# Gate/up results turned by DMA transposes on 16-bit planes instead of by TensorE

## The chip, the cores and the metric

One Trainium2 chip, one of its cores. The metric is the device time of one execution in microseconds, of which the median over several runs is taken. The program is compiled once; its weights lie in HBM and stream through the core's SBUF during the execution. TensorE (PE) multiplies, VectorE (DVE) and ScalarE (ACT) prepare its operands and take its results, SyncE (SP) issues most DMAs, ScalarE and GpSimd (POOL) issue some from their own queues. Each engine runs its instructions strictly in program order and waits on semaphores.

## The reference, cut to what matters

One layer of an encoder with 512 tokens and 2048 channels in fp32: two attention mixers side by side, an output projection, then a SwiGLU feed-forward of width 5632 (44 columns of 128) and a final RMSNorm. The change touches the hand-over inside the feed-forward:

```python
h2 = rmsnorm(x, g_ffn[layer])
gate, up = jnp.split(jnp.einsum('bsd,df->bsf', h2, w_gate_up[layer]), 2, axis=-1)
x = x + jnp.einsum('bsf,fd->bsd', jax.nn.silu(gate) * up, w_down[layer])
```

`silu(gate) * up` comes out with tokens on the partitions, and the product with `w_down` needs it with its 5632 columns on the partitions. It has to be turned, in blocks of 128 by 128.

## The kernel before, in words

**Products.** Every fp32 product is made from two-part operands: a value is split into a rounded first half (`hi`, by ScalarE, a Copy to the matmul's fp32r type) and the rest (`lo`, by VectorE, a subtraction), and `mm3` (lines 220 to 224) adds three matmuls, hi x hi, hi x lo and lo x hi. On top of that, `ColBlock` (line 841) uses a 2 x 2 block scheme with seven products instead of eight. The seven are called forms, `m1` to `m7`; each takes a sum of activation blocks (made ahead, in `arena`) and a sum of weight blocks (made when needed: `weights`, line 874, a VectorE step on two `raw` tiles, line 878).

**Units.** The program is a list of units. In the gate/up stage a unit is one form of one pair of 128 rows: six matmuls of 128 x 512. For unit n the generator emits, in this order: `prepare(n)` (line 1375), which loads weights for units up to `COLS_LOAD` = 20.0 planned us ahead and emits the splits of units up to `COLS_AHEAD` = 8.0 planned us ahead (a unit is planned at 1.37 us, so up to n + 5); the matmuls of unit n; and then the functions hooked to n. For each unit, `split_hi` (line 812) first makes the weight sum if the form needs one, then ScalarE writes the first half into the next `tw` pair (line 815); VectorE writes the second half (line 818), one unit behind the first halves. There are 8 `tw` pairs in turn (`TWINS`), so a first half waits until TensorE has finished the unit eight before.

**A gate/up block** (`gate_up_block`, line 1107) takes four of the 44 columns for gate and up, all 512 tokens, in 7 forms x 8 pairs = 56 units, in the order m1, m7, m6, m2, m5, m4, m3 (the first block has a part of it moved). Forms m7, m6, m5 and m4 need weight sums, m1, m2 and m3 do not. There are eleven blocks, one behind the other, then the down stage. The results gather in PSUM banks; `snap` copies them out after m1, m7 and m6 (line 1119, ScalarE), `add` adds m2, m5 and m4 (line 1126, VectorE), `silu` follows (line 1134), and after m3 `low` (line 1140) and `high` (line 1144) form the products `silu(gate) * up` of the two halves of the tokens, in the tiles `glo` and `uhi` (128 tokens x 512 columns, two tiles each).

**The turning** comes after m3, while TensorE is already in the next block: `turn(k)` for the four columns k, hooked to 6, 8, 18 and 20 units after the block's last unit. Each is four TensorE transposes of 128 x 128 into one bank (line 1151) and a copy of the bank by ScalarE (line 1154) into `pair`. Two columns make a pair; two units later `pair_sums` (four VectorE steps, line 353) forms the sums that the down stage's forms need, and `store` (line 1158) writes the seven forms to HBM from SP's queue. There is one `pair` tile, so the second pair's copies wait for the first one's store.

**Tiles.** Most tiles of the gate/up stage come from one set of interchangeable places, taken by `slot` (line 88, tag "s"); a tile waits for the last reader of what lay there before. Weights lie in `raw` tiles, 24 in the gate/up blocks.

Of the kernel before, what the change touches and what calls it, by code (L numbers as in the profile page):

```python
# [11 lines left out]
F32 = mybir.dt.float32  # L12
BF16 = mybir.dt.bfloat16
F32R = mybir.dt.float32r
AF = mybir.ActivationFunctionType
OP = mybir.AluOpType
AX = mybir.AxisListType
# [2 lines left out]
P = 128  # L20
# [51 lines left out]
def encoder_block(ctx, tc, x, w_in, g_q_a, g_k_a, w_out, w_gate_up, w_down, g_final, x_t, gains, c_ident, c_mask,  # L72
# [156 lines left out]
    units = []  # L229
    twins, evs, frs = [], [], []  # L230

    def in_turn(tiles, n, shape, dtype, tag):
        if not tiles:
            at_once = n if homing[0] else n // 2 if n == TWINS else 1
            for _ in range(n // at_once):
                whole = sp.tile([P, at_once] + shape[1:], dtype, tag=f"{tag}{at_once}", bufs=n // at_once, name=nm(tag))
                tiles.extend(whole[:, i] for i in range(at_once))
        tiles.append(tiles.pop(0))
        return tiles[-1]

# [743 lines left out]
    def out_chunk(kind, c):  # L984
        box = {}
        base = 0 if kind == "A" else NHA
        order = [6, 7, 0, 1, 2, 3, 4, 5] if (kind, c) == ("B", NC - 1) else list(range(NHA))

        def early(k):
            if (kind, k) not in oS and k >= SPILLED[kind]:  # L990
                drain_until(lambda: (kind, k) in oT)
                oS[kind, k] = split(oT.pop((kind, k)), "oS", go[:, base + k:base + k + 1],
                                    at=O_HOMES[kind][2 * k:2 * k + 2] if kind == "A" or k < 7 else None)

        class Back:
# [12 lines left out]
            def split_lo(self):  # L1008
                hi, lo = oS[kind, self.k]
                nc.vector.scalar_tensor_tensor(lo, self.t, go[:, base + self.k:base + self.k + 1], f32(hi),  # L1010
                                               op0=OP.mult, op1=OP.subtract)

        def mm(u, n):
            k = order[n]
            if n == 0:
                box["ps"] = [bank() for _ in range(NT)]
                if kind == "A":
                    x1[c] = [slot("x1") for t in range(NT)]
                    for t in range(NT):
                        nc.sync.dma_start(x1[c][t], x[0, t * P:(t + 1) * P, c * 512:(c + 1) * 512])  # L1020
            by_rows(u, n, NHA, lambda i, w, t: mm3(box["ps"][t], cols(oS[kind, order[i]], t * P), w, i == 0,
                                                   i == NHA - 1), post, kind == "A")

        def post(rows):
            drain_until(lambda: kind in ro)
            if (kind, c) == ("B", 0) and 0 in rows:
                nc.scalar.activation(slot("table")[:, :1], ones, AF.Silu)
            for t in rows:
                nc.vector.scalar_tensor_tensor(x1[c][t], box["ps"][t], ro[kind][:, t:t + 1], x1[c][t],
                                               op0=OP.mult, op1=OP.add)  # L1030
                release(box["ps"][t])
                if kind == "B" and c < NC - 1:
                    square_x1(c, t)
            if kind == "B" and NT - 1 in rows:
                wait(2 if c == 0 else 1)
                if c == NC - 1:
                    side.extend(lambda p=p: h_side(2 * c, p, True) for p in range(4))
                    side.append(lambda: [square_x1(c, t) for t in (0, 1)])
                    side.extend(lambda p=p: h_side(2 * c + 1, p, True) for p in range(2))
                    side.append(lambda: park_x1(c))  # L1040
                    side.append(lambda: [square_x1(c, t) for t in (2, 3)])
                    side.extend(lambda p=p: h_side(2 * c + 1, p, True) for p in range(2, 4))
# [64 lines left out]
    def gate_up_block(f0):  # L1107
        box = ColBlock(w_gate_up, 0, (f0 * P, DFF + f0 * P), KD // 2, REREAD, "craw40" if f0 == 40 else "craw", hf if f0 == 0 else None)
        st = {}

        def tile2(name):
            st[name] = slot(name, F32, (P, 2, 512))
            return st[name]

        def snap(form, name):
            def go():
                d = tile2(name)
                for t in range(2):
                    nc.scalar.activation(d[:, t], box.bank_of(form)[t], AF.Copy)
            box.after(form, 0, go)  # L1120

        def add(form, late, src, name):
            def go():
                d = st[name] = st.pop(src)
                for t in range(2):
                    nc.vector.tensor_tensor(d[:, t], box.bank_of(form)[t], d[:, t], op=OP.add)  # L1126
                if form in LAST_OF_BANK:
                    box.done(form)
            box.after(form, late, go)

        def silu(form, late, name, half):
            def go():
                for t in range(2):
                    nc.scalar.activation(st[name][:, t], st[name][:, t], AF.Silu,
                                         scale=r2["r"][:, 2 * half + t:2 * half + t + 1])
            box.after(form, late, go)

        def low():
            for t in range(2):
                nc.vector.tensor_tensor(st["glo"][:, t], box.bank_of("m3")[t], st["glo"][:, t], op=OP.mult)  # L1140
            box.done("m3")

        def high():
            nc.vector.tensor_tensor(st["uhi"], st["uhi"], st["ghi"], op=OP.mult)

        def turn(k):
            ps = bank()
            half = k % 2
            for n, t in enumerate((2, 3, 0, 1) if half == 0 else range(NT)):
                src = st[("glo", "uhi")[t // 2]][:, t % 2, k * P:(k + 1) * P]  # L1150
                nc.tensor.transpose(ps[:, n * P:(n + 1) * P], src, ident)  # L1151
# [24 lines left out]
        return box  # L1176

    for f in range(0, NFF, 4):
# [309 lines left out]
```

## Time and profile before

| | |
|---|---|
| median of 3 runs | 1971.99 us (1970.7 to 1972.68) |
| profiled execution, whole | 1972.09 us |
| its span, first to last instruction | 1970.3 us |
| the eleven gate/up blocks end | between 759 and 1541 us |
| TensorE, VectorE, ScalarE busy in 1072 to 1150 us (about one block) | 78.0, 63.4, 41.3 of 78 us |

The page gives busy times of each engine, the span in 40 slices, and the chain of work that ended last. Rows of groups read: line, engine, operation, tile written <- tiles read, partitions x elements, count | busy time, mean ns of one | idle time before it and what ended it. In a timeline, a row gives the start, the length, and the instruction; instructions that follow each other are put together with their count (x2), and overlap a little, so that two of them take less than twice one. The row of a window gives its length, then for each engine the busy time and (in brackets) the instructions, then the granted TensorE clock, the DMA engines' busy share and GB/s. Rows on DMA issues give the queue, the count, the size of each and the median us from issue to landing.

### The profile page before, as it was taken

How to read it: one execution, taken by the hardware profiler on the slowest of the kernel's cores; microseconds unless marked ns; L12 is line 12 of the kernel's file. 1: busy time of each engine (PE TensorE's matmuls, PEld its weight loads, DVE VectorE, ACT ScalarE, POOL GpSimd, SP SyncE). 2: the span in 40 equal slices, each digit the busy share in tenths (PEclk: the TensorE clock that was granted, in tenths of full speed). 3: DMA queues.
4: the chain of work that ended last, by engine and by line, in shares of the span. 5: the costliest groups of instructions: out<-in, count | busy, mean ns of one | idle time of the engine just before them, and what ended most of it. 6: DMA issues, size and time to landing. Idle time of an engine off the chain costs nothing.

```text
span 1970.3 us, 27367 instructions
## 1 busy us (share of the span) xinstructions
PE 1958.3 (99%) x8903; PEld 1615.1 (82%) x8903; DVE 1590.8 (81%) x2727; ACT 1126.1 (57%) x2045; POOL 120.3 (6%) x162
## 2 busy tenths in 40 slices
PE   9999999999999999999999999999999999999998
PEld 7888887888888888888888888888888888888886
DVE  7987678787775797787878878878879988878877
ACT  7755554565555565555554555545555666656655
POOL 0000011000000000000000000000000121111121
PEclk9999999999999999999999999999999999999999
DMA  9677683243343573754846737657457798869865
GB/s 343 234 258 235 211 272 111 69 138 124 131 148 119 183 240 130 275 197 172 299 137 221 275 123 259 226 171 276 160 193 273 205 270 247 233 144 265 236 131 167
DMA packets 230929, 399.01 MB, mean 203 GB/s; under 512 B 22785, under 2 KB 69633, under 8 KB 230657
## 3 DMA queue, kind: packets, MB, share of 16 engines
q1 hardware_dynamic: 205232, 330.84, 49.9%
q0 software_dynamic: 17200, 40.38, 9.4%
q10 hardware_dynamic: 8352, 26.05, 4.0%
q8 instruction: 69, 1.13, 0.2%
q14 instruction: 76, 0.61, 0.1%
HBM read 334.52 MB, written 62.65 MB: 202 GB/s over the span
## 4 chain that ended last, share of the span: by engine, by line
PE 92%; DVE 4%; ACT 1%; issue 1%; DMA 1%; ACTq 0%; DVEq 0%; POOLq 0%; SPq 0%; POOL 0%
PE b L222 30%; PE b L224 30%; PE b L223 30%; PE b L587 1%; PE b L1151 1%; DVE tw L818 1%; DMA raw<-in_w_down_dram 0%; DMA fr<-forms 0%; DVE raw L878 0%; PE b L1075 0%; DVE w L280 0%; PE b L537 0%; DVE arena L1202 0%; ACT tw L815 0%; DVE ra L434 0%
## 5 line engine op out<-in xcount | busy, mean ns | idle before, releaser
L222 PE MATMUL b<-tw,arena 128*128 128x512 f32 x2244 | 878.1, 391 | 0.6 <-ACT ev L1223 0.6
L223 PE MATMUL b<-tw,arena 128*128 128x512 f32 x2244 | 873.6, 389 | 0.6 <-DVE tw L818 0.6
L224 PE MATMUL b<-tw,arena 128*128 128x512 f32 x2244 | 874.0, 389 | 0.0
L815 ACT ACTIVATE tw<-raw 128x512 fp32r<-128x512 f32 x924 | 557.2, 628 | 426.5 <-DVE raw L878 290.8
L818 DVE TENSOR_TENSOR tw<-raw,tw 128x512 fp32r<-128x512 f32 x924 | 620.4, 686 | 161.9 <-ACT tw L815 151.9
L223 PEld LDWEIGHTS b<-tw,arena 128*128 128x128 f32 x2244 | 421.4, 188 | 88.1 <-DVE tw L818 1.7
L224 PEld LDWEIGHTS b<-tw,arena 128*128 128x128 f32 x2244 | 421.2, 188 | 88.4 <-DVE arena L321 0.4
L222 PEld LDWEIGHTS b<-tw,arena 128*128 128x128 f32 x2244 | 421.3, 188 | 87.7 <-ACT ev L1223 1.3
L878 DVE TENSOR_TENSOR raw<-raw,raw 128x512 f32<-128x512 f32 x528 | 360.9, 684 | 1.9 <-DMA raw<-in_w_gate_up_dram 1.9
L1224 POOL DMA_DIRECT2D x1d<-ev x76 | 66.3, 968 | 1144.5 <-ACT ev L1223 1127.4
L815 ACT ACTIVATE tw<-stage 128x512 fp32r<-128x512 f32 x140 | 85.4, 628 | 69.4 <-DVE stage L878 45.0
L818 DVE TENSOR_TENSOR tw<-stage,tw 128x512 fp32r<-128x512 f32 x140 | 93.8, 687 | 22.6 <-ACT tw L815 21.8
L222 PE MATMUL b<-w,arena 128*128 128x512 f32 x240 | 95.7, 399 | 0.0
L213 ACT ACTIVATE pTh<-b 128x512 fp32r<-128x512 f32 x64 | 38.2, 598 | 98.0 <-PE b L587 94.3
L224 PE MATMUL b<-w,arena 128*128 128x512 f32 x240 | 93.9, 391 | 0.0
L223 PE MATMUL b<-w,arena 128*128 128x512 f32 x240 | 93.5, 390 | 0.0
L1223 ACT ACTIVATE ev<-b,fixed 128x512 f32<-128x512 f32 x76 | 49.8, 682 | 29.1 <-PE b L224 27.3
L353 DVE TENSOR_TENSOR pair<-pair 128x256 f32<-128x256 f32 x120 | 45.5, 421 | 23.6 <-ACT pair L1078 22.6
L1126 DVE TENSOR_TENSOR s<-b,s 128x512 f32<-128x512 f32 x66 | 44.0, 687 | 24.7 <-PE b L224 24.7
L1154 ACT ACTIVATE pair<-b 128x512 f32<-128x512 f32 x44 | 26.3, 597 | 48.9 <-PE b L1151 48.6
L224 PEld LDWEIGHTS b<-w,arena 128*128 128x128 f32 x240 | 45.0, 188 | 10.0
L223 PEld LDWEIGHTS b<-w,arena 128*128 128x128 f32 x240 | 45.2, 188 | 9.1
(223 smaller groups left out, 1779.5 us busy)
## 6 DMA issues: line engine op xcount, KB each, us to landing
raw<-in_w_gate_up_dram SPq DMA_DIRECT2D x616, 256.0 KB, 5.3
raw<-in_w_down_dram SPq DMA_DIRECT2D x176, 256.0 KB, 6.4
stage<-in_w_in_dram SPq DMA_DIRECT2D x111, 256.0 KB, 5.3
forms<-pair SPq DMA_DIRECT2D x22, 896.0 KB, 5.3
x1d<-ev POOLq DMA_DIRECT2D x76, 256.0 KB, 6.5
fr<-forms ACTq DMA_DIRECT2D x35, 512.0 KB, 4.5
raw<-in_w_out_dram SPq DMA_DIRECT2D x32, 512.0 KB, 4.9
stage<-in_w_in_dram SPq DMA_DIRECT2D x90, 128.0 KB, 3.4
```

Source lines behind the costliest of these rows:

```text
L213: nc.scalar.activation(hi, src, AF.Copy)
L222: nc.tensor.matmul(dst, ah, bh, start=start, stop=False, skip_group_check=chained)
L223: nc.tensor.matmul(dst, ah, bl, start=False, stop=False, skip_group_check=chained)
L224: nc.tensor.matmul(dst, al, bh, start=False, stop=stop, skip_group_check=chained)
L353: nc.vector.tensor_tensor(out, x, y, op=op)
L815: nc.scalar.activation(self.pair[:, 0], self.src, AF.Copy)
L818: nc.vector.tensor_tensor(self.pair[:, 1], self.src, f32(self.pair[:, 0]), op=OP.subtract)
L878: nc.vector.tensor_tensor(t[dst], t[src[0]], t[src[1]], op=OP.add if form == "m6" else OP.subtract)
L1126: nc.vector.tensor_tensor(d[:, t], box.bank_of(form)[t], d[:, t], op=OP.add)
L1154: nc.scalar.activation(st["pair"][:, half * 1024:half * 1024 + 512], ps, AF.Copy)
L1223: nc.scalar.activation(e, box.bank_of(form)[t], AF.Copy, scale=r2["r"][:, row:row + 1])
L1224: nc.gpsimd.dma_start(x1_dram[2 * cb + j, row], e, accum_op=OP.add)
```

## The change

The transposes leave TensorE. `planes` (ScalarE) copies each of the four 128 x 512 results as 16-bit words, so that the lower and the upper words of each pair of columns lie apart (1024 words a partition), and issues from ScalarE's own DMA queue a transpose from SBUF to SBUF, 128 x 1024 words into 8 blocks of 128 x 128 (in the built program, tiles of 16 rows by 128 columns, so 64 a transfer). `merge(j)` (ScalarE, three copies) interleaves the words of two turned columns into `pair`. `planes` stands 2 and 4 units after the block's end, `merge` 9 and 19. `pair_sums` follows one unit after its merge, `store` six.

With that, three other things change. The `tw` pairs are single tiles from the attention stage on (class `Pair`), where they were cut from two tiles of four pairs each. Results and residuals (`s1` to `uhi`) are single 128 x 512 tiles rather than tiles of two, so `high` becomes two steps; the residual `x1` becomes one tile of four instead of four. And one of the 21 `raw` buffers of the first two column blocks of the down stage goes (`draw6` 21 to 20), which makes room.

```diff
-RAWS = {"raw": 6, "craw": 24, "craw0": 24, "kraw": 9, "craw40": 18, "draw6": 21, "draw8": 28}
+RAWS = {"raw": 6, "craw": 24, "craw0": 24, "kraw": 9, "craw40": 18, "draw6": 20, "draw8": 28}
...
+    class Pair:
+        def __init__(self):
+            self.parts = [sp.tile([P, 512], F32R, tag="tw", bufs=2 * TWINS, name=nm("tw")) for _ in range(2)]
+
+        def __getitem__(self, at):
+            return self.parts[at[1]]
...
         def tile2(name):
-            st[name] = slot(name, F32, (P, 2, 512))
+            st[name] = [slot(name) for t in range(2)]
             return st[name]
...
         def high():
-            nc.vector.tensor_tensor(st["uhi"], st["uhi"], st["ghi"], op=OP.mult)
-
-        def turn(k):
-            ps = bank()
-            half = k % 2
-            for n, t in enumerate((2, 3, 0, 1) if half == 0 else range(NT)):
-                src = st[("glo", "uhi")[t // 2]][:, t % 2, k * P:(k + 1) * P]
-                nc.tensor.transpose(ps[:, n * P:(n + 1) * P], src, ident)
+            for t in range(2):
+                nc.vector.tensor_tensor(st["uhi"][t], st["uhi"][t], st["ghi"][t], op=OP.mult)
+
+        def planes(name, half):
             if half == 0:
-                st["pair"] = sp.tile([P, 4 * 512], F32, tag="pair", bufs=1, name=nm("pair"))
-            nc.scalar.activation(st["pair"][:, half * 1024:half * 1024 + 512], ps, AF.Copy)
-            release(ps)
+                st["turned"] = sp.tile([P, NT, 2, 2, 2, P], U16, tag="turned", bufs=1, name=nm("turned"))
+            for t in range(2):
+                halves = slot("planes", U16, (P, 2, 2, 256))
+                src = st[name][t].bitcast(U16).rearrange("p (j c s) -> p j s c", j=2, s=2)
+                nc.scalar.activation(halves, src, AF.Copy)
+                nc.scalar.dma_start_transpose(st["turned"][:, 2 * half + t].rearrange("p j s f c -> p (j s f) c"),
+                                              halves.rearrange("p j s c -> p (j s c)"))
+            st.pop(name)
+
+        def merge(j):
+            pair = st["pair"] = sp.tile([P, 4 * 512], F32, tag="pair", bufs=1, name=nm("pair"))
+            turned = st["turned"][:, :, j].rearrange("p t s f c -> p f t c s")
+            for f, lo, hi, at in ((0, 2, 4, 0), (0, 0, 2, 256), (1, 0, 4, 1024)):
+                dst = pair[:, at:at + (hi - lo) * P].bitcast(U16).rearrange("p (t c s) -> p t c s", c=P, s=2)
+                nc.scalar.activation(dst, turned[:, f, lo:hi], AF.Copy)
...
-        for k in range(4):
-            late = (6, 8, 18, 20)[k]
-            box.after("m3", late, lambda k=k: turn(k))
-            if k % 2:
-                box.after("m3", late + 2, lambda: pair_sums(st["pair"]))
-                box.after("m3", late + 7, lambda k=k: store((f0 + k) // 2))
+        for late, name, half in ((2, "glo", 0), (4, "uhi", 1)):
+            box.after("m3", late, lambda name=name, half=half: planes(name, half))
+        for j, late in enumerate((9, 19)):
+            box.after("m3", late, lambda j=j: merge(j))
+            box.after("m3", late + 1, lambda: pair_sums(st["pair"]))
+            box.after("m3", late + 6, lambda j=j: store(f0 // 2 + j))
```

In the changed kernel the lines after 231 have other numbers: the splits are at 825 and 828, the weight sums at 888, the snaps at 1130, `low` at 1151, `high` at 1156, the plane copies at 1164, the transposes at 1165, the merges at 1174, `pair_sums` at 363, the store at 1177.

How ScalarE's program moves, after the end of the second block. Before (`tw` is a split of a coming unit, the snap of m1 is line 1119):

```order
L1154 ACTIVATE pair_7323<-b_74 128x512
L815 ACTIVATE tw_5865<-raw_7223 128x512
L815 ACTIVATE tw_5866<-raw_7235 128x512
L1154 ACTIVATE pair_7323<-b_73 128x512
L1119 ACTIVATE s_690_7348<-b_78 128x512
L1119 ACTIVATE s_690_7348<-b_77 128x512
L815 ACTIVATE tw_5866<-raw_7247 128x512
```

Now, first the planes, four units or more earlier than the first eviction was (the two splits between them are those of the next block's units 8 and 9):

```order
L1164 ACTIVATE planes_7292<-s_638_6710 128x1024
L1165 DMA_TRANSPOSE turned_7291<-planes_7292 128x8x128
L1164 ACTIVATE planes_7295<-s_639_6711 128x1024
L1165 DMA_TRANSPOSE turned_7291<-planes_7295 128x8x128
L825 ACTIVATE tw_5867<-raw_7181 128x512
L825 ACTIVATE tw_5853<-raw_7193 128x512
L1164 ACTIVATE planes_7317<-s_647_6807 128x1024
L1165 DMA_TRANSPOSE turned_7291<-planes_7317 128x8x128
L1164 ACTIVATE planes_7320<-s_648_6808 128x1024
L1165 DMA_TRANSPOSE turned_7291<-planes_7320 128x8x128
```

and then, after the splits of units 10 to 13, the snap and the first merge, between the splits of units 13, 14 and 15:

```order
L825 ACTIVATE tw_5861<-raw_7243 128x512
L1130 ACTIVATE s_707_7359<-b_78 128x512
L1130 ACTIVATE s_708_7360<-b_77 128x512
L825 ACTIVATE tw_5863<-raw_7255 128x512
L1174 ACTIVATE pair_7372<-turned_7291 128x512 x2
L1174 ACTIVATE pair_7372<-turned_7291 128x1024
L825 ACTIVATE tw_5865<-raw_7267 128x512
```

Ten instructions now stand on ScalarE (planes and merges, and four DMA issues besides) where four evictions stood, and the merge's three stand in one piece. In the built program the fourth planes tile takes the place of the second (so its copy waits for the second transpose to land), and the two m1 snaps take the places of the fourth and the third (so they wait for those transposes).

On VectorE, the same place. Before, the pair sums stand behind the second half of unit 14:

```order
L818 TENSOR_TENSOR tw_5866<-raw_7247,tw_5866 128x512
L353 TENSOR_TENSOR pair_7323<-pair_7323 128x256 x4
L878 TENSOR_TENSOR raw_7273<-raw_7271,raw_7273 128x512
L818 TENSOR_TENSOR tw_5866<-raw_7259,tw_5866 128x512
L878 TENSOR_TENSOR raw_7185<-raw_7185,raw_7100 128x512
```

Now:

```order
L828 TENSOR_TENSOR tw_5864<-raw_7255,tw_5863 128x512
L363 TENSOR_TENSOR pair_7372<-pair_7372 128x256 x4
L888 TENSOR_TENSOR raw_7281<-raw_7279,raw_7281 128x512
L828 TENSOR_TENSOR tw_5866<-raw_7267,tw_5865 128x512
L888 TENSOR_TENSOR raw_7193<-raw_7193,raw_7108 128x512
```

They stand in the same place: the pair sums behind the second half of unit 14, then the sum of unit 16 and the second half of unit 15. The second pair sums stand behind the second half of unit 24 (before, behind that of unit 26).

More of the change, by code (lines that the diff above doesn't have):

```diff
@@ L14 @@
 F32R = mybir.dt.float32r
+U16 = mybir.dt.uint16
 AF = mybir.ActivationFunctionType
@@ L230, in encoder_block @@
     twins, evs, frs = [], [], []
-    def in_turn(tiles, n, shape, dtype, tag):
+    class Pair:
[3 more added lines that the diff above has]
+            return self.parts[at[1]]
+    def in_turn(tiles, n, shape, dtype, tag):
+        if not tiles and homing[0]:
+            whole = sp.tile([P, n] + shape[1:], dtype, tag=tag + "s", bufs=1, name=nm(tag))
+            tiles.extend(whole[:, i] for i in range(n))
+        if not tiles and tag == "tw":
+            tiles.extend(Pair() for _ in range(n))
         if not tiles:
[L234 to L237, printed above, removed]
+            tiles.extend(sp.tile(shape, dtype, tag=tag, bufs=n, name=nm(tag)) for _ in range(n))
         tiles.append(tiles.pop(0))
@@ L1017, in mm @@
                 if kind == "A":
-                    x1[c] = [slot("x1") for t in range(NT)]
+                    whole = slot("x1", F32, (P, NT, 512))
+                    x1[c] = [whole[:, t] for t in range(NT)]
                     for t in range(NT):
@@ L1118, in go @@
                 for t in range(2):
-                    nc.scalar.activation(d[:, t], box.bank_of(form)[t], AF.Copy)
+                    nc.scalar.activation(d[t], box.bank_of(form)[t], AF.Copy)
             box.after(form, 0, go)
@@ L1125, in go @@
                 for t in range(2):
-                    nc.vector.tensor_tensor(d[:, t], box.bank_of(form)[t], d[:, t], op=OP.add)
+                    nc.vector.tensor_tensor(d[t], box.bank_of(form)[t], d[t], op=OP.add)
                 if form in LAST_OF_BANK:
@@ L1133, in go @@
                 for t in range(2):
-                    nc.scalar.activation(st[name][:, t], st[name][:, t], AF.Silu,
+                    nc.scalar.activation(st[name][t], st[name][t], AF.Silu,
                                          scale=r2["r"][:, 2 * half + t:2 * half + t + 1])
@@ L1139, in low @@
             for t in range(2):
-                nc.vector.tensor_tensor(st["glo"][:, t], box.bank_of("m3")[t], st["glo"][:, t], op=OP.mult)
+                nc.vector.tensor_tensor(st["glo"][t], box.bank_of("m3")[t], st["glo"][t], op=OP.mult)
             box.done("m3")
         def high():
-            nc.vector.tensor_tensor(st["uhi"], st["uhi"], st["ghi"], op=OP.mult)
-        def turn(k):
-            ps = bank()
-            half = k % 2
-            for n, t in enumerate((2, 3, 0, 1) if half == 0 else range(NT)):
-                src = st[("glo", "uhi")[t // 2]][:, t % 2, k * P:(k + 1) * P]
-                nc.tensor.transpose(ps[:, n * P:(n + 1) * P], src, ident)
-            if half == 0:
-                st["pair"] = sp.tile([P, 4 * 512], F32, tag="pair", bufs=1, name=nm("pair"))
-            nc.scalar.activation(st["pair"][:, half * 1024:half * 1024 + 512], ps, AF.Copy)
-            release(ps)
+            for t in range(2):
+                nc.vector.tensor_tensor(st["uhi"][t], st["uhi"][t], st["ghi"][t], op=OP.mult)
+        def planes(name, half):
+            if half == 0:
+                st["turned"] = sp.tile([P, NT, 2, 2, 2, P], U16, tag="turned", bufs=1, name=nm("turned"))
[12 more added lines that the diff above has]
+                nc.scalar.activation(dst, turned[:, f, lo:hi], AF.Copy)
         def store(n):
```

## The prediction

> **What bounds the kernel now.** I read the page's busy shares first, then the chain of waits in the gate/up stage, then TensorE's timeline at one place, then VectorE's and ScalarE's at the end of a block.
>
> ```profile
> span 1970.3 us, 27367 instructions
> ...
> PE 1958.3 (99%) x8903; PEld 1615.1 (82%) x8903; DVE 1590.8 (81%) x2727; ACT 1126.1 (57%) x2045; POOL 120.3 (6%) x162
> ...
> PEclk9999999999999999999999999999999999999999
> ```
> ```profile
> PE b L222 <- ACT ev L1223: 0.6, 1, 0.6
> ```
> ```profile
> by line: PE b L223 32.5%; PE b L222 32.3%; PE b L224 32.3%; PE b L1151 3.1%
> ...
> 1001.73 0.44 PE b L1151 x4
> ```
> TensorE is busy 99% of the span at the full clock, and its waits come to 0.6 us in this row and hardly more elsewhere. Between 1000 and 1100 us the chain is TensorE alone, and the four transposes of line 1151 are a link in it: 3.1% of it. So TensorE's work is the time, and its removal is a gain as long as nothing else falls behind.
>
> What a group of four transposes takes is read from the starts around it:
>
> ```profile
> 766.83 0.39 PE L223 MATMUL b<-tw,arena 128*128 128x512 f32 x1
> 767.06 0.39 PE L224 MATMUL b<-tw,arena 128*128 128x512 f32 x1
> 767.29 0.60 PE L1151 MATMUL b<-fixed,s 128*128 128x128 f32 x4
> 767.65 0.48 PE L222 MATMUL b<-tw,arena 128*128 128x512 f32 x1
> 767.96 0.40 PE L223 MATMUL b<-tw,arena 128*128 128x512 f32 x1
> 768.20 0.40 PE L224 MATMUL b<-tw,arena 128*128 128x512 f32 x1
> ```
> ```profile
> L1140 DVE TENSOR_TENSOR s<-b,s x22: 678/692/692, 758.6 to 1540.5; 128x512 f32<-128x512 f32 x22
> ```
> From 767.06 to 768.20 are 1.14 us for three steps that take 0.228 each without transposes, so a group costs 0.456 us. The second row checks it: it has two steps a block, 0.6 us apart, so the eleven blocks end (1540.5 - 0.6 - 758.6) / 10 = 78.1 us apart, which is 56 units of six matmuls at 1.363 and 4 groups at 0.456. One unit is taken as 1.365 us (6 x 0.2275) below.
>
> **What the change removes.** 44 groups (4 in each of 11 blocks), 44 x 0.456 = **20.1 us** of TensorE. No wait goes, so nothing is "late next" at once; the question is whether ScalarE and VectorE still deliver each unit's `tw` pair in time.
>
> **What it adds to ScalarE.** In one block: four plane copies (1024 elements) and six merge copies (four of 512, two of 1024), for four evictions of a bank that go (each the size of line 1119's, 1.08 us for two).
>
> ```profile
> L815 ACT ACTIVATE tw<-raw 128x512 fp32r<-128x512 f32 x924 | 557.2, 628 | 426.5 <-DVE raw L878 290.8 <-PE b L224 108.6 <-DMA raw<-in_w_gate_up_dram 10.0
> ```
> ```profile
> L364 ACT ACTIVATE rows<-rows x8: 1045/1046/1053, 32.7 to 69.6; 128x1024 f32<-128x1024 f32 x8
> ```
> ```profile
> 1084.01 1.08 ACT L1119 ACTIVATE s<-b 128x512 f32<-128x512 f32 x2
> 1084.96 1.16 ACT L815 ACTIVATE tw<-raw 128x512 fp32r<-128x512 f32 x2
> ```
> ```profile
> 1072.00:1150.00 78.00, 78.00 (x353) 64.58 (x352) 63.35 (x106) 41.25 (x71) 0.00 (x0) 1.00 0.62 213
> ```
> No row has a 16-bit copy with strides; I take the float copies of the same length: 0.63 us for 512 elements, 1.05 for 1024, and a step of 0.53 where 512s follow each other (1.16 for two). Planes 4 x 1.05 = 4.2, merges 2 x 2.1 to 2.3 = 4.4, less 2 x 1.08 = 2.2: 6.4 us more, on 41.25 in 78 (the window's ACT column). As an average that is nothing. But a `tw` pair goes through ScalarE (first half) and then VectorE (second half), VectorE's program is at most a unit behind ScalarE's, and both run in order; so what counts is the stretch in which ScalarE is held.
>
> **Two prices that the trace does not show:** D, for which the ScalarE queue is held to issue one transpose, and L, from its issue to its landing.
>
> ```profile
> L1196 ACTq DMA_DIRECT2D fr<-forms x42: 326/326/362, 1462.2 to 1840.9; - x42
> ```
> ```profile
> L1224 POOL DMA_DIRECT2D x1d<-ev x76 | 66.3, 968 | 1144.5 <-ACT ev L1223 1127.4 <-ACT tw L815 7.9 <-DMA fr<-forms 7.9
> ```
> ```profile
> raw<-in_w_gate_up_dram SPq DMA_DIRECT2D x616, 256.0 KB, 5.3
> ...
> vB<-ends ACTq DMA_DIRECT2D x2, 256.0 KB, 3.8
> ...
> qkB<-ends ACTq DMA_DIRECT2D x2, 256.0 KB, 2.0
> ```
> ```profile
> 1071.00:1076.00 5.00, 5.00 (x23) 4.14 (x23) 4.98 (x8) 1.19 (x2) 0.00 (x0) 1.00 0.02 3
> ...
> 1081.00:1088.00 7.00, 7.00 (x34) 5.77 (x33) 4.83 (x10) 3.55 (x7) 0.00 (x0) 1.00 0.00 0
> ```
> D lies between 0.33 (a plain DMA on the same queue) and 0.97 (the longest kind of issue, GpSimd's); I take 0.33, its own queue's row. L for 256 KB lies between 2.0 (this queue) and 5.3 (a weight load with others ahead of it). After a block's end the DMA engines are nearly empty (shares 0.02 and 0.00 in these windows), which speaks for the lower rows; I take 3.0, the middle of the queue's own 2.0 and 3.8. Nothing excludes values under either lower bound, but they bring no gain beyond the 20.1.
>
> [...]
>
> **The chain at a block's end, with time zero where TensorE ends the block** (1071.0 in the trace), unit k being the k-th of the next block:
>
> ```profile
> 1071.02 1.37 DVE L1140 TENSOR_TENSOR s<-b,s 128x512 f32<-128x512 f32 x2 [1.99 <-PE b L224]
> 1072.31 1.28 DVE L818 TENSOR_TENSOR tw<-raw,tw 128x512 fp32r<-128x512 f32 x2
> 1073.51 1.22 DVE L1144 TENSOR_TENSOR s<-s,s 128x1024 f32<-128x1024 f32 x1
> 1074.65 0.68 DVE L878 TENSOR_TENSOR raw<-raw,raw 128x512 f32<-128x512 f32 x1
> ...
> 1086.24 1.55 DVE L353 TENSOR_TENSOR pair<-pair 128x256 f32<-128x256 f32 x4
> 1087.71 0.68 DVE L878 TENSOR_TENSOR raw<-raw,raw 128x512 f32<-128x512 f32 x1
> 1088.31 0.68 DVE L818 TENSOR_TENSOR tw<-raw,tw 128x512 fp32r<-128x512 f32 x1
> ```
> VectorE goes at 0.6 us a step (1087.71 to 1088.31), 1.2 for a unit that needs a weight sum, against TensorE's 1.365: it wins 0.165 a unit. Today the second half of unit 15 (the last row) is ready at 18.0; TensorE wants it at 0.07 + 14 x 1.365 + 2 x 0.456 = 20.1. The margin is 2.1 us, and without transposes 1.2.
>
> In the changed order ScalarE does: planes 1 from 0.74 (first `low` product) to 1.79, issue to 2.1; planes 2 to 3.25, issue from 3.3 to 3.63; split 8 to 4.28; split 9 once VectorE has its sum (`low`, two halves, the two steps of `high`, the sum: 4.4), to 5.08; planes 3 to 6.03, issue to 6.43. Planes 4 lies in the slot of planes 2 and waits for that transpose: 3.3 + L = 6.3, just hidden; to 7.5, issue from 7.55 to 7.88. Split 10 ends at 8.53. Then VectorE paces: second halves 10 to 13 start at 8.55, 9.75, 10.95, 12.15. ScalarE's two m1 snaps wait for TensorE (10.9) and for transposes 4 and 3, whose sources lie in their slots (7.55 + L = 10.55): 11.65 to 12.75. Split 14 to 13.3, first merge 0.53 + 0.53 + 1.05 to 15.4. VectorE: pair sums 15.45 to 16.95, a sum, second half 15 to **18.2**, wanted at **19.2**: margin 1.0. Nine units on it is 1.0 + 9 x 0.165 = 2.5 for unit 24; there the second merge (2.1), the pair sums (1.55) and unit 25's half (0.6, less pipelining 0.65 in all) take 3.6 together, and unit 25 is wanted 1.365 later: margin 2.5 + 1.37 - 3.6 = **0.2**. So the work hides behind TensorE, barely: the cover at unit 25 is a fifth of a microsecond, at unit 15 one.
>
> If cover is gone: each 1 us of D costs up to 4 us, since four issues stand in the chain, the first two partly hidden until D = 0.43; late by 2(D - 0.33) + (2D - 0.85). Each 1 us of L over 3.15 delays planes 4 by 1, and over 4.15, where the snap waits too, costs 2. Once unit 15 has no margin, unit 25 adds 0.7 (1.5 + 1.37 - 3.6).
>
> **Edits that I cost at nothing.** `high` as two steps is 0.07 us longer on VectorE, in the chain above. The separate `tw` and `s` tiles wait for the same last readers. Each transpose also waits for the DMA eight issues before it (weight loads, long landed in the idle window), and later weight loads on SP's queue wait for transposes; they run some 14 units, 19 us, ahead, against landings of 3 to 5. The store of the forms is issued at the same unit for the first pair and two units earlier for the second. One `draw6` buffer fewer lets a few loads of two column blocks go a unit later: 0 to 3 us, as the chain there runs through loads already. The eleventh block ends in the down stage, where VectorE has little room:
>
> ```profile
> 1541.00:1560.00 19.00, 19.00 (x89) 15.74 (x88) 18.26 (x31) 11.30 (x20) 2.99 (x4) 1.00 0.35 67
> ```
> 18.26 of 19 busy: 0 to 4 us once. For these two I take 1 us together.
>
> **The sum,** against the profiled execution's own 1972.1 (span 1970.3 and 1.8 around it; the median of the runs is 1972.0, so no correction): 1972.1 - 20.1 + 1 = **1953.0**.
>
> **Rivals.** First, slower: the ScalarE queue is held by each issue. It decides from D = 0.9 on, where 2 x 0.57 + 0.95 - 1.0 + 0.7 = 1.8 us a block eats the 1.82 that the block saves. At D = 0.97: 1.4 + 0.7 = 2.1, +3 us, 1975; at 1.5, over every row, 4.2, +26, 1998. For it: no row shows a transposing issue, and each has 64 tiles to hand out. [...] Against: this queue's 42 issues all took 326 to 362 ns. Chance 0.13.
>
> Second, slower or even: landing. At L = 5.3 it stalls 2 x 1.15 + 0.7 = 3.0 a block, +13 us, 1985; even at 4.7; at 3.8 it stalls 0.4 at unit 25 only, 1957. For it: the 5.3 of most 256 KB loads. Against: the empty engines in those windows. [...] Chance of L over 4.5: 0.12.
>
> Third, a partial gain: D of 0.5 to 0.8, L of 3.5 to 4.5, or both merges a little longer than their float rows, 0.3 to 1.5 us a block: 1956 to 1969. Chance 0.20.
>
> **Chances and range.** The forecast (1950 to 1957) 0.55, partial 0.20, the slow ones 0.25, of which 0.07 end within 0.2% (3.9 us, about what a measurement of this kernel can tell from no change). Of the partial, 0.02 ends there too. So faster 0.73, same 0.09, slower 0.18. The low end is the whole 20.1 with 2 us for what the slots' new places may give; the high end, 1977, leaves out the last 0.17 or so.
>
> **What would show it.** Right: no transposes on TensorE, block ends 76.3 us apart, TensorE's waits for `tw` under 0.3 us a block; ACTq's issues near 0.33 us, landings near 3; plane copies near 1.05. Wrong: waits of TensorE for the second half of `tw` some 15 or 25 units after a block's end; which price is at fault is read from the length of the issues, or from ScalarE's idle time before planes 4 and before the snaps.

## The result, and the profile after

The changed kernel is slower: 2004.02 us (median of 4 runs, 2003.53 to 2004.76) against 1971.36 of the kernel before in the same runs, a ratio of 1.0165 (95% interval 1.0148 to 1.0183). The forecast was 1953.0. TensorE did lose its transposes (8903 matmuls before, 8727 now), and yet the span grew by 32.7 us. The head of the page, then TensorE's waits (total, times, longest), then VectorE's `low`, two steps at each of the eleven block ends:

```profile
span 2003.0 us, 27133 instructions
...
PE 1959.2 (98%) x8727; PEld 1601.8 (80%) x8727; DVE 1591.1 (79%) x2738; ACT 1193.2 (60%) x2111; POOL 120.4 (6%) x162
```
```profile
PE b L224 <- DVE tw L828: 21.5, 26, 1.8
PE b L223 <- ACT tw L825: 4.7, 6, 1.6
PE b L223 <- ACT ev L1242: 4.5, 3, 2.7
```
```profile
L1151 DVE TENSOR_TENSOR s<-b,s x22: 683/692/692, 760.1 to 1566.7; 128x512 f32<-128x512 f32 x22
```

Before, the wait for `ev` took 0.6 us (the row in the prediction), and those for `tw` as much:

```profile
PE b L223 <- DVE tw L818: 0.6, 2, 0.3
```

So 1.2 us of such waits have become over 30. The block ends lie (1566.7 - 0.6 - 760.1) / 10 = 80.6 us apart; before it was 78.1, and the forecast 76.3. The 32.7 us of the span fall into three parts: 1.5 us before the first block's end (760.1 against 758.6), 24.7 in the ten periods, 6.5 behind the last block's end (2003.0 - 1566.1 = 436.9 against 1970.3 - 1539.9 = 430.4).

The two prices that the prediction had to guess are now rows. The issues of the transposes (least, median and longest), and at the end the time from issue to landing:

```profile
L1165 ACTq DMA_TRANSPOSE turned<-planes x44: 1247/1249/2231, 761.9 to 1577.0; - x44
...
  ACT planes L1164: 14.6, 8
  ACT s L1130: 1.8, 1
...
DMA to landing us min/median/max: 3.0/4.4/7.0
```

D, the hold of ScalarE's queue for one issue, is 1.25 us (taken: 0.33, upper bound 0.97). L is 4.4 us at the median (taken: 3.0). What this does is seen on ScalarE behind the block end that lies at 1082.7 (the start of `low`, the prediction's time zero; ACTq is ScalarE's DMA queue, in brackets the idle time of the engine ahead of the instruction, which contains its own issues):

```profile
1083.46 1.06 ACT L1164 ACTIVATE planes<-s 128x1024 uint16<-128x1024 uint16 x1 [0.78 <-DVE s L1151]
1084.55 1.25 ACTq L1165 DMA_TRANSPOSE turned<-planes  x1
1085.84 1.06 ACT L1164 ACTIVATE planes<-s 128x1024 uint16<-128x1024 uint16 x1 [1.33 <-DVE tw L828]
1086.93 1.28 ACTq L1165 DMA_TRANSPOSE turned<-planes  x1
1088.31 1.15 ACT L825 ACTIVATE tw<-raw 128x512 fp32r<-128x512 f32 x2 [1.41 <-PE b L225]
1089.37 1.04 ACT L1164 ACTIVATE planes<-s 128x1024 uint16<-128x1024 uint16 x1
1090.44 1.29 ACTq L1165 DMA_TRANSPOSE turned<-planes  x1
1091.78 1.06 ACT L1164 ACTIVATE planes<-s 128x1024 uint16<-128x1024 uint16 x1 [1.37 <-DMA turned<-planes]
1092.87 1.25 ACTq L1165 DMA_TRANSPOSE turned<-planes  x1
1094.21 1.16 ACT L825 ACTIVATE tw<-raw 128x512 fp32r<-128x512 f32 x2 [1.38 <-PE b L224]
```

Between 1083.46 and 1094.21 ScalarE makes two splits where TensorE uses up eight units. VectorE runs dry behind it, catches up at 1.2 us a unit, and then has to wait for the merge as well:

```profile
1090.79 0.69 DVE L888 TENSOR_TENSOR raw<-raw,raw 128x512 f32<-128x512 f32 x1
1094.88 0.69 DVE L828 TENSOR_TENSOR tw<-raw,tw 128x512 fp32r<-128x512 f32 x1 [3.41 <-ACT tw L825]
...
1101.86 1.56 DVE L363 TENSOR_TENSOR pair<-pair 128x256 f32<-128x256 f32 x4 [1.47 <-ACT pair L1174]
1103.33 0.69 DVE L888 TENSOR_TENSOR raw<-raw,raw 128x512 f32<-128x512 f32 x1
1103.93 0.69 DVE L828 TENSOR_TENSOR tw<-raw,tw 128x512 fp32r<-128x512 f32 x1
```

That last second half, of unit 15, is ready at 1104.6, 21.9 us behind the block's end, where the prediction had 18.2. TensorE is there first, and stands; these are its steps:

```profile
1102.40 0.49 PE L223 MATMUL b<-tw,arena 128*128 128x512 f32 x1
1104.67 0.50 PE L224 MATMUL b<-tw,arena 128*128 128x512 f32 x1 [1.78 <-DVE tw L828]
```

2.27 us for a step of 0.227: 2.04 us lost. In nine of the ten periods the step at unit 15 is that long, to within 0.01.

A second loss sits behind the first. After the same wait in the next block (columns of the second view: window, length, busy time of PE, PEld, DVE, ACT and POOL with counts, granted clock, DMA share, GB/s):

```profile
1183.89 0.50 PE L224 MATMUL b<-tw,arena 128*128 128x512 f32 x1 [1.78 <-DVE tw L828]
...
1185.66 0.63 PE L224 MATMUL b<-tw,arena 128*128 128x512 f32 x1
1186.09 0.63 PE L225 MATMUL b<-tw,arena 128*128 128x512 f32 x1
```
```profile
1180.00:1185.00 5.00, 3.22 (x14) 2.21 (x13) 3.89 (x9) 2.66 (x4) 0.00 (x0) 1.00 0.22 76
1185.00:1190.00 5.00, 5.00 (x17) 3.92 (x16) 5.00 (x10) 2.69 (x6) 0.00 (x0) 0.66 1.00 315
```

About one microsecond after the wait TensorE's steps take 0.43 instead of 0.227 for some 3.4 us: the granted clock is half (0.50 in a window from 1185.2 to 1188.4, 0.66 over the window of 5). That happens in five of the ten periods and costs 1.4 to 1.7 us each. The other five have a wait of the same length without a drop of the clock behind it; what decides is not shown.

Counted step by step over the ten periods (806.0 us, against 761.6 at the full gain of 76.16 that the runs below show): steps that the trace marks as waits are 30.5 us too long, steps at half the clock 7.7, other lengthened steps, most of them beside the waits, 5.2; 1.0 is left over. The longest period is the last (84.58 us): 8.4 of the 44.4 lie there.

### The profile page after: what moved, and what is told of

Same layout as the page of the kernel before. It is cut to its first block, busy times and chain, and to the rows that moved or that the text cites. A ratio compares the mean times of both kernels' runs of the same rounds, so it can differ in the third digit from the quotient of the medians.

```text
span 2003.0 us, 27133 instructions
## 1 busy us (share of the span) xinstructions
PE 1959.2 (98%) x8727; PEld 1601.8 (80%) x8727; DVE 1591.1 (79%) x2738; ACT 1193.2 (60%) x2111; POOL 120.4 (6%) x162
## 4 chain that ended last, share of the span: by engine, by line
PE 76%; DVE 8%; ACT 6%; DMA 4%; issue 3%; ACTq 2%; POOL 0%; DVEq 0%; SPq 0%; POOLq 0%
PE b L224 25%; PE b L225 25%; PE b L223 24%; DVE tw L828 2%; DVE raw L888 2%; ACT pair L1174 2%; ACTq L1165 2%; ACT planes L1164 2%; DMA turned<-planes 1%; PE b L597 1%; ACT tw L825 1%; DVE pair L363 1%; DMA raw<-in_w_in_dram 1%; ACT s L1130 1%; DMA x<-x1d 0%
## 5 line engine op out<-in xcount | busy, mean ns | idle before, releaser
L825 ACT ACTIVATE tw<-stage 128x512 fp32r<-128x512 f32 x140 | 85.4, 628 | 69.4 <-DVE stage L888 44.4
L828 DVE TENSOR_TENSOR tw<-stage,tw 128x512 fp32r<-128x512 f32 x140 | 93.9, 688 | 21.9 <-ACT tw L825 21.8
L1164 ACT ACTIVATE planes<-s 128x1024 uint16<-128x1024 uint16 x44 | 46.4, 1054 | 42.7 <-DMA turned<-planes 13.3
```

The costliest lines, as they stand in the source:

```text
L825: nc.scalar.activation(self.pair[:, 0], self.src, AF.Copy)
L828: nc.vector.tensor_tensor(self.pair[:, 1], self.src, f32(self.pair[:, 0]), op=OP.subtract)
L1164: nc.scalar.activation(halves, src, AF.Copy)
```

## The experiments

Five theories. A: the issue holds ScalarE, and with it the splits. B: the landings do it, through the slots that planes 4 and the snaps wait for. C: ScalarE's copies are too long by themselves. E: the other tiles and the missing `draw6` buffer cost what is lost outside the ten periods. F, a rival to A formed later: it is the transposing transfers, not the hold. Two more, G and H, are about the last period alone and come with their runs. All times are medians; the ratio is to the kernel before on the same chip.

| run | hold of ScalarE a plane, us | time, us | ratio (95% interval) | first block end | mean period of ten |
|---|---|---|---|---|---|
| before | none | 1971 to 1972 | 1 | 758.6 | 78.13 |
| changed | 1.25 | 2004.0 | 1.0165 (1.0148 to 1.0183) | 760.1 | 80.60 |
| sp_queue | none | 1960.8 | 0.9947 (0.9932 to 0.9961) | 760.8 | 76.65 |
| own_slots | 1.25, fourth up to 3.5 | 2009.2 | 1.0193 (1.0178 to 1.0208) | 759.8 | 81.55 |
| layout_alone | none | 1975.2 | 1.0025 (1.0015 to 1.0035) | 760.0 | 78.11 |
| plain_dma | 0.47 | 1962.1 | 0.9951 (0.9936 to 0.9966) | 761.3 | 76.59 |
| plain_x2 | 1.12 | 1995.3 | 1.0125 (1.0110 to 1.0140) | 762.1 | 79.70 |
| plain_x3 | 1.78 | 2022.2 | 1.0261 (1.0245 to 1.0276) | 760.2 | 82.10 |
| no_turn | none | 1951.5 | 0.9904 (0.9888 to 0.9921) | 757.7 | 76.16 |
| sp_spread | none | 1958.1 | 0.9937 (0.9922 to 0.9952) | 759.8 | 76.62 |
| act_spread | 1.25, three units apart | 1978.4 | 1.0039 (1.0025 to 1.0054) | 761.2 | 77.62 |
| sp_late | none | 1960.8 | 0.9951 (0.9936 to 0.9966) | 761.9 | 76.74 |
| layout_21 | none | 1973.7 | 1.0011 (1.0002 to 1.0021) | 760.3 | 78.10 |
| hybrid | none | 1959.7 | 0.9934 (0.9921 to 0.9948) | 761.5 | 76.39 |

**sp_queue.** One word changes: who issues.

```diff
-                nc.scalar.dma_start_transpose(
+                nc.sync.dma_start_transpose(
```

> Only the issuing queue of the 44 transposes changes, ScalarE's for SyncE's. Theory A (the issue of 1.25 us, four a block, holds ScalarE and so the split of the weights): ScalarE's program is back to what the prediction had with D near 0, the 2.04 us wait some 15 units after each block's end shrinks under 0.5, and the clock drops that follow it go: 1958 to 1972 us (2004 less most of the 43 us that ten blocks lost against 76.3 us each). Theory B (landing: planes 4 and the snaps wait for transposes 2 to 4 because of their slots, L is 4.4): the landing is not earlier, so the loss stays: 1990 to 2005. Theory C (the copies by ScalarE, 4 x 1.06 and 2 x 2.34 a block, are too long by themselves): 1995 to 2005.

Measured 1960.8: A's number, and faster than both kernels. ScalarE's timeline behind a block's end (at 1065.4), and the transposes on SyncE's queue:

```profile
1066.15 2.01 ACT L1164 ACTIVATE planes<-s 128x1024 uint16<-128x1024 uint16 x2 [0.77 <-DVE s L1151]
1068.06 0.61 ACT L825 ACTIVATE tw<-raw 128x512 fp32r<-128x512 f32 x1
1069.91 0.63 ACT L825 ACTIVATE tw<-raw 128x512 fp32r<-128x512 f32 x1 [1.24 <-DVE raw L888]
1070.45 1.99 ACT L1164 ACTIVATE planes<-s 128x1024 uint16<-128x1024 uint16 x2
1072.35 1.14 ACT L825 ACTIVATE tw<-raw 128x512 fp32r<-128x512 f32 x2
```
```profile
L1165 SPq DMA_TRANSPOSE turned<-planes x44: 1231/1282/2190, 762.6 to 1534.5; - x44
...
DMA to landing us min/median/max: 3.1/3.2/4.9
```

The two splits that began 11.5 us behind the block's end begin 6.9 behind it. Nine of the ten periods are 76.16 us, without one wait for `tw`, and no period has a clock drop. The copies are the same, so C falls. But the landing fell too, from 4.4 to 3.2 us (the weight loads now stand behind the transposes in one queue; in the changed kernel's eleventh block, where the last three transposes have no other DMA beside them, the four land in 3.0 to 3.1 us as well); so this run alone does not part A from B.

**own_slots.** The planes get buffers that nothing else uses, so no instruction waits for a landing because of a slot.

```diff
-                halves = slot("planes", U16, (P, 2, 2, 256))
+                halves = sp.tile([P, 2, 2, 256], U16, tag="planes", bufs=4, name=nm("planes"))
```

> The four tiles of planes get buffers of their own, so neither planes 4 nor the snaps wait for a transpose to land; the issues stay on ScalarE's queue. Theory B: most of the loss goes, 1960 to 1980. Theory A: in most blocks planes 4 waits less than 0.1 us behind the issue of transpose 3, so only the waits of 3.6, 1.8 and 1.5 us of single blocks go, and what they cost: 1996 to 2003. Theory C: as now, 2002 to 2005.

Measured 2009.2, slower still, which no theory had. The waits for the slots are gone, but:

```profile
1093.30 1.25 ACTq L1165 DMA_TRANSPOSE turned<-planes  x1
1094.59 1.06 ACT L1164 ACTIVATE planes<-s 128x1024 uint16<-128x1024 uint16 x1 [1.33 <-issue]
1095.68 3.54 ACTq L1165 DMA_TRANSPOSE turned<-planes  x1
1099.33 1.15 ACT L825 ACTIVATE tw<-raw 128x512 fp32r<-128x512 f32 x2 [3.67 <-PE b L225]
```

In seven of eleven blocks the fourth issue takes 2.3 to 3.5 us; in the one shown the second and third transposes land only 9.1 and 7.0 us after their issue began. With earlier transposes still under way the issue itself was held here: in all seven blocks the long issue ends within 0.6 us of the second transpose's landing. B as it was put falls: the slot was not what ScalarE waited for. A late landing cost all the same here, by making the next issue longer (2.3 to 3.5 us instead of 1.25), so it is a part of A's hold.

**layout_alone.** The changed kernel with TensorE's `turn` and the hooks of before (6, 8, 18, 20) put back; the tiles and `draw6` stay as changed.

> The changed kernel with TensorE's transposes and their evictions put back, with the hooks of before: what is left of the change is the tiles that it cuts differently (tw and s one by one, x1 whole) and 20 instead of 21 buffers of draw6. Theory A, and B and C with it: the new places cost nothing in the gate/up stage: 1971 to 1974. Theory E (the changed kernel's losses outside the ten block periods, 1.5 us ahead of the first and 6.5 us in the down stage, come from the new places and the missing buffer): 1978 to 1980.

Measured 1975.2, between A's number and E's. The span of the profiled run is 2.2 us longer than before: 1.4 ahead of the first block's end, and 1.0 behind the last (1972.5 - 1541.1 = 431.4), with the periods unchanged. Over all runs the ratio makes it 3 to 7 us; the profiled run is one of the shorter ones. Ahead of the first block this kernel has one wait of TensorE, in the attention stage, that before doesn't have and the changed kernel does (1.6 us there):

```profile
PE b L597 <- DVE pTl L215: 1.5, 1, 1.5
```

So E explains the 1.5 us in front, and perhaps 1.0 of the 6.5 behind. The other 5.5 go in sp_queue, whose end also takes 1958.7 - 1527.3 = 431.4: they are the hold again, in the eleventh block. The sizes are rough. Behind the last block the runs in which ScalarE is held 0.47 us a plane or not at all take 428.9 to 433.2 us, those with 1.12 or more 435.8 to 439.2.

**plain_dma.** Plain DMAs of the same bytes on ScalarE's queue; the kernel leaves the turning out.

```diff
-                nc.scalar.dma_start_transpose(...(j s f) c"), halves.rearrange("p j s c -> p (j s c)"))
+                nc.scalar.dma_start(...(j s f) c"), halves.rearrange("p j s (f c) -> p (j s f) c", c=P))
```

> The transposes become plain DMAs of the same bytes from the same queue (the turning is left out, so the planes land unturned); the ten ScalarE copies a block and every wait stay. Theory A: the issue falls to 0.33 us, ScalarE gets back 3.7 us a block, the stall is near what the prediction had: 1953 to 1965. Theory B: landing decides; if these land in 3 us as predicted, 1953 to 1962, if in over 4.4, 1985 or more. Theory C: the copies are unchanged, 1995 to 2004.

```profile
L1165 ACTq DMA_DIRECT2D turned<-planes x44: 472/472/513, 763.1 to 1535.8; - x44
...
  ACT planes L1164: 7.6, 9
...
DMA to landing us min/median/max: 2.2/3.5/5.1
```

Measured 1962.1, with 0.47 us an issue and a landing of 3.5. It fits A, and since planes 4 still waits for landings in 9 blocks at no cost to TensorE (no period but the last has a wait of TensorE), it speaks against B. F, that transposes load the DMA engines, was still open.

**plain_x2 and plain_x3** part A from F: the same plain DMAs, each plane in two or three pieces, so that ScalarE is held longer without any transpose.

```diff
+                cuts = (0, 4, 8)
+                for lo, hi in zip(cuts, cuts[1:]):
+                    nc.scalar.dma_start(dst[:, lo:hi], src[:, lo:hi])
```

In plain_x3 the cuts are 0, 3, 6, 8.

> Plain DMAs in place of the transposes (turning left out), each plane in two of half the size, all on ScalarE's queue: the queue is held 2 x 0.47 = 0.94 us a plane instead of 0.47, with no transposing transfer anywhere. Theory A (holding ScalarE is what costs): by the prediction's own slope, 2 x 0.61 + 1.03 - 1.0 + 0.7 = 2 us a block, 1975 to 1985, with waits of TensorE some 15 units behind each block's end. Theory F (it is the transposing transfers, which fill the DMA engines and land late): as with plain DMAs in one piece, 1960 to 1965.

> The same in three pieces a plane: 3 x 0.47 = 1.41 us, a little more than the 1.25 of a transposing issue. Theory A: stalls as in the changed kernel or over it, with clock drops behind them: 1995 to 2015. Theory F: 1960 to 1967.

The hold of one plane in each, from the timelines:

```profile
1083.80 1.12 ACTq L1169 DMA_DIRECT2D turned<-planes  x2
```
```profile
1088.05 1.78 ACTq L1169 DMA_DIRECT2D turned<-planes  x3
```

Measured 1995.3 and 2022.2. The pieces took 0.56 and 0.61 us at the median, not 0.47, so the holds are 1.12 and 1.78 instead of 0.94 and 1.41, and both runs are slower than expected. F falls: without a transposing transfer anywhere the loss is back. The changed kernel's 2004.0 at 1.25 lies between its neighbours 1995.3 at 1.12 and 2022.2 at 1.78 (the straight line gives 2000.6). At 1.12 the step at unit 15 is 2.18 to 2.27 us long in nine of ten periods, nearly as in the changed kernel.

**no_turn.** The kernel before without the 176 transposes; the evictions read the products, so this kernel leaves the turning out too.

```diff
-                nc.tensor.transpose(ps[:, n * P:(n + 1) * P], src, ident)
...
-            nc.scalar.activation(st["pair"][:, half * 1024:half * 1024 + 512], ps, AF.Copy)
+            src = st[("glo", "uhi")[half]][:, k // 2]
+            nc.scalar.activation(st["pair"][:, half * 1024:half * 1024 + 512], src, AF.Copy)
```

> The kernel before without TensorE's transposes: the four evictions a block read the products themselves, so nothing is turned and pair sums and stores get unturned data. It shows what 20.1 us less of TensorE is worth when nothing is added. If the removal is worth what the prediction had: 1951 to 1953, all blocks 76.2 apart. If VectorE (18.3 of 19 us busy behind the last block) becomes the bound there, as one reading of the 81.1 us of that block in the kernel with SyncE's queue has it: 1954 to 1958, with the last block 78 or more. If that block's loss comes from the merges instead: 1951 to 1953.

Measured 1951.5, with all ten periods at 76.16, the last among them: the removal is worth what the prediction said, and VectorE is no bound in that last period.

```profile
L1140 DVE TENSOR_TENSOR s<-b,s x22: 691/692/692, 757.7 to 1520.0; 128x512 f32<-128x512 f32 x22
```

**sp_spread.** sp_queue stays 8 us above the forecast, and 4.9 of them lie in the last period (81.1 us). Here each merge is four copies, hooked one unit apart, with the pair sums at +4 and the store at +9.

> Transposes on SyncE's queue, and each merge cut into four copies of 512 that are hooked one unit apart, the pair sums one unit behind the last. Theory G (what is left in the last block, 81.1 us for it, is VectorE idle for 1.5 us ahead of each pair sum because three merge copies in a row hold up the split): that block comes to 77 to 79, 1955 to 1959. Against it (VectorE has no room there whatever ScalarE does): 1960 to 1963.

Measured 1958.1, but the last period is 80.8: the time fits, the reason doesn't. G falls. What VectorE waits for there is not the merge; it is a weight load:

```profile
DVE raw L888 <- DMA raw<-in_w_gate_up_dram: 4.6, 4, 3.0
```

In no_turn that wait is 0.6 us over the same stretch.

**sp_late.** All four transposes at 8 units behind the block's end in SyncE's program.

> As the one with merges spread out and SyncE's queue, but the four transposes are put in that queue's program 8 units behind the block's end instead of 2 and 4; they can start no later for it, as SyncE stands waiting for the planes up to 20 us in the last block. Theory H (the last block loses 4.6 us because the weight loads stand behind the transposes in SyncE's queue): that block comes to 77 to 78, 1953 to 1956. Against it (VectorE or the merges there): 1957 to 1960.

Measured 1960.8, the last period 81.9, the wait for loads 6.4 us. H in this form falls: putting the transposes later in the queue doesn't bring the loads earlier.

**hybrid.** As sp_spread, but the last two blocks are turned by TensorE (`if f0 >= 36`), with 21 `draw6` buffers.

> The first nine blocks turn by DMA from SyncE's queue with the merges spread out; the last two (whose turning falls among the loads for the down stage) are turned by TensorE as before, with 21 buffers of draw6. If the last interval's loss (80.8 us there) comes from what the DMA way does in that block: nine intervals of 76.2, the last at 78.2, 1953 to 1956. If the loss comes from the place and not from the way of turning: the last interval stays at 80 or more, 1957 to 1961.

The last period is 78.45, with VectorE's wait for loads at 0.6 us: it is the DMA way, in that block, that makes the loads late, and not the place. The 21st `draw6` buffer is not the reason: layout_alone has 20 and 78.24 us there. The total, 1959.7, is no better than sp_spread's: behind the last block's end it takes 1958.6 - 1525.4 = 433.2 us, against 1955.2 - 1526.0 = 429.2 in sp_spread, and its first block ends 1.7 us later; no cause is shown for either. How the loads come late there (SyncE's queue taken up by the four issues for 5.6 us in sp_late and 7.2 in sp_spread, or the transfers themselves) stays open.

**act_spread.** Back on ScalarE's queue, the holds as long as before, but one every third unit, the merges from 15 and 25 on.

```diff
+        for k in range(4):
+            box.after("m3", 2 + 3 * k, lambda k=k: planes(k))
-        for j, late in enumerate((9, 19)):
+        for j, late in enumerate((15, 25)):
```

> All four transposing issues stay on ScalarE's queue, 1.25 us each, but one plane and its issue every third unit (2, 5, 8 and 11 units behind the block's end), then the merges from units 15 and 25 on, a copy a unit. ScalarE's work is the same. Three units are 4.1 us of TensorE; a split of 0.53 for each and 2.3 for plane and issue are 3.9. If it is the stretch that costs (four issues inside ten units): most of the stall goes, 1956 to 1966. If it is the sum of ScalarE's time, or the transposing transfers: 1990 to 2005.

Measured 1978.4, between the two. Over the ten periods 14.6 us of 44.4 are left, 4.7 of them in the last one, as in sp_queue: most of the loss came from the stretch. The rest is not clean evidence, since the later merges bring a wait of their own, for the store of the pair before:

```profile
  DMA forms<-pair: 34.4, 10
```

**layout_21** is layout_alone with `draw6` 21.

> TensorE's transposes with the changed kernel's tiles, as in the run with the layout alone, but 21 buffers of draw6 again. If the missing buffer costs the 1.0 us behind the last block and the tiles the 1.4 us ahead of the first: the first block ends at 760.0 as there, the part behind the last block takes 430.4 as before instead of 431.4. If both come from the tiles: 760.0 and 431.4. 1972 to 1976 in either case, too near to tell by the time alone.

First block end 760.3, behind the last 1972.2 - 1541.3 = 430.9: the front belongs to the tiles; of the 1.0 behind, half went, which is too little to tell from chance.

## Why the prediction was wrong

- **The removal** (20.1 us) was right: no_turn is 19 to 22 us faster than before (by the ratio and by the spans), and with the transposes on SyncE's queue nine of ten periods are 76.16 as well.
- **The step that failed is D**: "I take 0.33, its own queue's row", with 0.97 as the upper bound. It is 1.25. The row was of the right queue but of another kind of DMA, and the bound was of another engine. The same bytes moved plainly took 0.47, so it is the turning that made the issue long here.
- **The chain was right.** With the measured D its own formula gives 2 x 0.92 + 1.65 - 1.0 + 0.7 = 3.2 us of stall a block; waits and lengthened steps in the trace are (30.5 + 5.2) / 10 = 3.6, or 3.3 without the last period. For plain_dma it gives about 0 (0.0 to 0.3 measured outside the last period), for plain_x2 2.7 (3.0, or 2.7 without the last period), for plain_x3 5.3 (4.9, or 4.6). The places were right as well: unit 15 in nine periods and unit 25 in five. In four periods TensorE waits at unit 10 too, for the split behind the fourth issue; the text had no wait there.
- **The first rival was the mechanism**, given 0.13. Its two values of D, 0.97 with 1975 and 1.5 with 1998, lie on either side of the measured 1.25, and the upper bound of 0.97 was nearer to it than the 0.33 that was taken. Both times are under the measured 2004, since the clock, the tiles and the eleventh block are not in them.
- **L** was mis-sized as well, 4.4 for 3.0; it was 3.2 in sp_queue, and 3.0 to 3.1 in the changed kernel's eleventh block. The "nearly empty" DMA engines were read from the kernel before; in the changed kernel five weight loads are issued 3 to 8 us behind the block's end, beside the transposes, and the share of the DMA engines (the last figure but one of the row) is 1.04:

```profile
1086.00:1089.00 3.00, 3.00 (x15) 2.50 (x14) 1.14 (x3) 1.59 (x3) 0.00 (x0) 1.00 1.04 257
```

L cost little in the changed kernel, since planes 4 begins 0.05 us behind the end of the third issue in the block shown. The wait of planes 4 for transpose 2, 14.6 us over the kernel, has the issue ahead of it in it (8 x 1.3), and its removal gained nothing.
- **The copies**: planes 1.05 as taken (the row at 1083.46 has 1.06); a merge 2.3, where the chain has 2.1.
- **What was missing**: the granted clock after a wait, 7.7 us over ten periods. No term of the sum had it.
- **Edits costed at nothing or 1 us**: the tiles cost 2.2 us of span (layout_alone; 3 to 7 by its ratio), and the eleventh block about 5.5, over the 0 to 4 of the text; there ScalarE's hold delays the evictions `ev` that TensorE waits for (2.7 us at once, with a clock drop behind it).

With the formula at D = 1.25, 1972.1 + 11 x (3.2 - 1.82) = 1987; add 4 for the formula's shortfall over ten periods (some 3 of it in the last), 7.7 for the clock, 2.5 for the tiles (1.5 in front, 1.0 behind) and 4 for the eleventh block (5.5, of which the formula has 1.4): 2005, against 2004 measured. The parts were measured after the fact, so this shows that little is missing, not that each is exact.

## What to carry to other kernels

A DMA cost the engine that issued it as well as the engines that moved it: one issue held its queue for 0.33 us (forms), 0.47 (a plain one of a plane) or 1.25 (a transposing one). So price the issue of each kind by a row of that kind. Where there is none, let the range reach well over the rows of other kinds: here they had 0.33 and 0.97, and the issue of 64 tiles took 1.25. Before moving work to an engine's queue, ask which engine's program has nothing behind it: the same transposes cost 43 us more on ScalarE's queue than on SyncE's. A margin of 1 us in a chain of 18 is no cover for a guessed price that occurs four times in it.

## What the runs showed of the hardware

- A transposing issue of 128 x 1024 16-bit words held its queue for 1.25 us on ScalarE and 1.23 to 1.28 on SyncE (least and median), and landed 3.2 us after its start at the median from SyncE's queue (sp_queue), 4.4 from ScalarE's (changed kernel; 3.0 to 3.1 in its eleventh block).
- With earlier transposes not yet landed, a fourth issue was held for 2.3 to 3.5 us (own_slots, seven blocks).
- TensorE's granted clock fell to 0.50 for some 3.4 us after waits of 1.5 to 1.8 us, in five of ten periods of the changed kernel and in eight of ten of own_slots. After a wait of 1.8 us in the other five of the changed kernel, and in one of own_slots, it did not fall.
